# Values spread by transposes, and sums over the features by transposes with row sums on VectorE, in two transformer blocks on one Trainium2 core

## The chip, the cores and the metric

The kernel runs on one core of one Trainium2 chip. The metric is the device time of one execution in microseconds, and less is better. A core has five engines that run their own instruction streams: TensorE (PE in the profile, with its weight loads as PEld), VectorE (DVE), ScalarE (ACT), GpSimd (POOL) and SyncE (SP), which here only starts transfers. TensorE writes only to PSUM, of which this kernel uses eight banks of 128 x 512 fp32.

## The reference

Two blocks run one after the other on x, 512 tokens with 1024 features, in fp32. The first has a forgetting-attention layer and a latent-attention layer, each followed by a squared-ReLU MLP, and a final norm; the second has a mixer with four branches and a gated convolutional feed-forward. What matters for this change are the norms, which all have one shape:

```python
def rms_norm(x, g):
    xf = x.astype(jnp.float32)
    y = xf * lax.rsqrt(jnp.mean(xf * xf, axis=-1, keepdims=True) + EPS)
    return (y * g.astype(jnp.float32)).astype(x.dtype)

def second_block(x, c, ...):
    ...
    h = rms_norm_2(x, tm_pre_g[l]) * (1.0 + sc_t) + sh_t
    y = token_mixer(h, w_in[l], ...)
    x = x + g_t * rms_norm_2(y, tm_post_g[l])
    h = rms_norm_2(x, cm_pre_g[l]) * (1.0 + sc_c) + sh_c
    y = conv_ffn(h, ffn_w_up[l], ffn_dw_w[l], ffn_w_down[l])
    x = x + g_c * rms_norm_2(y, cm_post_g[l])
```

`head_rms_norm`, which the mixer applies to two branches, is the same over groups of 64 features.

## The kernel before

**Layout.** An activation is kept as eight tiles of 128 features x 512 tokens (features on the partitions), and each is split into a high and a low part in fp32r. A product with a weight is three matmuls (`mm3`, lines 215 to 217). The weights come in chunks of 128 x 1024 over SP's queue, are split by ScalarE (L181) and VectorE (L182), and are taken in order by `take`.

**Sums and spreads.** With the features on the partitions, a norm needs a sum over partitions. `token_sum` (L277) has the squares summed over the tiles in one tile `ss` and multiplies each of its 128 x 128 pieces by a tile of ones in plain fp32 (L284): every column of the result holds the sum of 128 tokens, and one column of each piece is read back as 4 values a partition. VectorE scales it (L292), GpSimd takes the power -1/2 (L294). `spread` (L297) brings the 4 values a partition back over all features: a matmul of the broadcast column with the identity (L301), again fp32. `head_rms` (L864, L873) does the sum with a tile that has ones in two 64 x 64 blocks, `head_gain` (L879, L887) the spread for it.

**The mixer.** Its input h is not ready when its first projections start, so these use an earlier h and are corrected by a bias row: `bps`, gathered by L781 in the loop over k, is copied by ScalarE (L804) and turned by four small matmuls (L807). After this come the projections of the short convolution (`sc`), 24 `mm3` matmuls for each of 128 columns, in groups that share the loop over k.

**The start of the second feed-forward.** The tokens are treated in two halves, `HT[0]` and `HT[1]`, with 256-column matmuls in `half_mm`. `half_norms` is a generator: it is advanced by `step(norms)` between two `half_mm`, and does the norm after `w_o` (first `rsqrt_tok`, the residual in L1219 and L1220), the norm before the feed-forward (second `rsqrt_tok`, L1224) and the modulation (`modulate`, L782). `x_tokens` (L1237) turns x to tokens on the partitions by 32 transposes, for the residual at the end.

**Order.** Each engine executes its own instructions in order. The build may place an instruction ahead of others of its engine, so the order of the code is not always that of an engine; where the change speaks of order, rows of it are shown below. PSUM has two pools of four banks, `acc` and `att`; a matmul into a bank waits until the bank's last reader is done.

Of the kernel before, what the change touches and what calls it, by code (L numbers as in the profile page):

```python
# [13 lines left out]
ALU = mybir.AluOpType  # L14
# [5 lines left out]
EPS = 1e-6  # L20
# [66 lines left out]
def _body(ctx, tc, T, n_chunks, rec, dump):  # L87
    nc = tc.nc
    act, dve, pool, pe = nc.scalar, nc.vector, nc.gpsimd, nc.tensor
# [22 lines left out]
    def U(tag="tmp", dt=F32, w=S):  # L112
        if tag in BASE:
            return main.tile([128, w], dt, tag=tag, bufs=BASE[tag], name=tag)
        return phase["pool"].tile([128, w], dt, tag=tag, bufs=phase["tags"][tag], name=tag)
# [4 lines left out]
    def small(w, name="s"):  # L120
        return main.tile([128, w], F32, tag=f"s{w}", bufs=6, name=name)
# [12 lines left out]
    def C(name, w):  # L134
        o = _COFF[name]
        return cst[:, o:o + w]
# [13 lines left out]
    ident = C("ident", 128)  # L150
# [82 lines left out]
    def project(src, cols, X, bank=None):  # L233

        return group(src, [cols], X, bank)[0]

    def group(src, colss, X, bank=None):

        pss = [b() for b in (bank if isinstance(bank, tuple) else (bank or acc,) * len(colss))]
        for k in range(len(X)):  # L240
            for ps, cols in zip(pss, colss):
                wh, wl = take(src, k * 128, cols)
                mm3(ps[0:wh.shape[1]], wh, wl, X[k][0], X[k][1], k == 0, k == len(X) - 1)
        return pss
# [32 lines left out]
    def token_sum(sss):  # L277

        ps = att()
        w = sss[0].shape[1]  # L280
        for s in range(w // 128):
            xs = slice(s * 128, (s + 1) * 128)
            for i, ss in enumerate(sss):
                pe.matmul(ps[:, xs], lhsT=ss[:, xs], rhs=ones, start=i == 0, stop=i == len(sss) - 1)  # L284
        return ps[:, 0:w:128]

    def rsqrt_tok(ss, n, eps=EPS):

        ps = token_sum([ss])
        w = ps.shape[1]  # L290
        t = small(4, "mst")[:, 0:w]
        dve.tensor_scalar(out=t, in0=ps, scalar1=1.0 / n, scalar2=eps, op0=ALU.mult, op1=ALU.add)  # L292
        r = small(4, "rtok")[:, 0:w]
        pool.tensor_tensor(out=r, in0=t, in1=mhalf[:, 0:w], op=ALU.pow)  # L294
        return r

    def spread(rt, tag="tmp"):  # L297

        ps = att()
        for s in range(rt.shape[1]):  # L300
            pe.matmul(ps[:, s * 128:(s + 1) * 128], lhsT=rt[:, s:s + 1].to_broadcast([128, 128]), rhs=ident,  # L301
                      start=True, stop=True)
        if tag is None:
            return ps
        r = U(tag)
        act.activation(out=r, in_=ps, func=AF.Copy)
        return r
# [90 lines left out]
    x, h = [], []  # L398
    for k in range(KT):
        t = U("ctx")  # L400
# [43 lines left out]
    for a in range(2):  # L444
        p0 = 64 - 64 * a
        t = klc[a]
# [167 lines left out]
    ps = acc()  # L614
# [3 lines left out]
    us, ss = mult(pkv, rb2)  # L618
    h = [split_s(x[k], V("norm_mix_g", 8 + k), U2("v" if k < 4 else "h")) for k in range(KT)]
# [20 lines left out]
    us, ss = mult(pq, rb2)  # L640
# [77 lines left out]
    h = []  # L718
# [40 lines left out]
    def ct(name, i):  # L759
        return [(O[name] + 128 * i, 128)]  # L760
# [7 lines left out]
    pss = [acc() for _ in colss]  # L768
# [3 lines left out]
    for k in range(KT):  # L772
# [6 lines left out]
        o = st["slot"] * 128  # L779
# [16 lines left out]
    h = [modulate(k, x[k], rb_h, gG, sh_t, U2("h")) for k in range(KT)]  # L796
    x5d = ctx.enter_context(tc.tile_pool(name="x5d", bufs=1, space=bass.MemoryType.DRAM)).tile([D, S], F32, name="x5d")
    for k in range(KT):
        dve.scalar_tensor_tensor(out=x[k], in0=x[k], scalar=V("final_norm_g", k), in1=rb_f, op0=ALU.mult, op1=ALU.mult)
        nc.scalar.dma_start(out=x5d[k * 128:(k + 1) * 128], in_=x[k])  # L800
        dump(f"x5_{k}", x[k])

    brow = U()
    act.activation(out=brow[0:2], in_=bps[0:2], func=AF.Copy)  # L804
    bps = att()
# [11 lines left out]
    gq, gk = [], []  # L817
    for ps, out, c, b in ((pss[1], gq, 0.125, 10), (pss[2], gk, 1.0, 4), (pss[3], gq, 0.125, 14)):
        t = U("mix")
# [10 lines left out]
    def keep(ps, scale=1.0, tag="tmp"):  # L830
        t = U(tag)
        act.activation(out=t, in_=ps, func=AF.Copy, scale=scale)
        return t
# [30 lines left out]
    def head_rms(hs):  # L864

        t = small(16, "hms")
        for p in range(2):
            ps = att()
            q = U()
            act.activation(out=q, in_=hs[p], func=AF.Square)  # L870
            for s in range(4):
                xs = slice(s * 128, (s + 1) * 128)
                pe.matmul(ps[:, xs], lhsT=q[:, xs], rhs=C("half", 128), start=True, stop=True)  # L873
            dve.tensor_scalar(out=t[:, 8 * p:8 * p + 8], in0=ps[:, 0::64], scalar1=1.0 / 64, scalar2=EPS, op0=ALU.mult, op1=ALU.add)
        r = small(16, "hr")
        pool.tensor_tensor(out=r, in0=t, in1=mhalf, op=ALU.pow)
        return r

    def head_gain(hs, r, gname, gate):  # L879

        out = []
        for p in range(2):
            ps = att()
            re = U()
            dve.tensor_copy(out=re.rearrange("p (a b) -> p a b", a=8), in_=r[:, 8 * p:8 * p + 8].unsqueeze(2).to_broadcast([128, 8, 64]))
            for s in range(4):
                pe.matmul(ps[:, s * 128:(s + 1) * 128], lhsT=re[:, s * 128:(s + 1) * 128], rhs=ident, start=True, stop=True)  # L887
            dve.tensor_tensor(out=hs[p], in0=ps, in1=hs[p], op=ALU.mult)
            dve.scalar_tensor_tensor(out=hs[p], in0=hs[p], scalar=V(gname, p), in1=gate[p], op0=ALU.mult, op1=ALU.mult)
            out.append(split(hs[p], U2("y")))  # L890
        return out
# [8 lines left out]
    for p in range(2):  # L900
        ps = att()
# [6 lines left out]
        scan(gB[p], z, ALU.add)  # L908


    pss = group("w_in_2", [ct("gla_k", 1), ct("sc", 4), ct("sc", 2), ct("sc", 5)], h, (att, att, acc, acc))
    gk.append(keep(pss[0], 1.0, "mix"))
    xv = [keep(pss[1]), keep(pss[3])]
    scu = [ph.tile([128, 2 + S], F32, tag="cv", bufs=2, name=f"scu{p}") for p in range(2)]
    for p in range(2):
        dve.tensor_copy(out=scu[p][:, 0:2], in_=zero[:, 0:2])
    dve.tensor_tensor(out=scu[0][:, 2:], in0=pss[2], in1=xv[0], op=ALU.mult)
    pss = group("w_in_2", [ct("sc", 3), ct("sc", 0), ct("sc", 1)], h)
    dve.tensor_tensor(out=scu[1][:, 2:], in0=pss[0], in1=xv[1], op=ALU.mult)
    yin = {3: []}  # L920
    for p in range(2):
        o = U()
        dve.tensor_scalar(out=o, in0=scu[p][:, 0:S], scalar1=V("sc_dw_w_2", p), scalar2=None, op0=ALU.mult)
        for j in (1, 2):
            dve.scalar_tensor_tensor(out=o, in0=scu[p][:, j:j + S], scalar=V("sc_dw_w_2", 2 * j + p), in1=o, op0=ALU.mult, op1=ALU.add)
        dve.tensor_tensor(out=o, in0=pss[1 + p], in1=o, op=ALU.mult)
        dump(f"sc_{p}", o)
        yin[3].append(split(o, U2("y")))

# [138 lines left out]
    pss = group("w_in_2", [ct("ml_o", 0), ct("ml_o", 1)], h)  # L1068
# [17 lines left out]
    ps = att()  # L1086
# [7 lines left out]
    for p in range(2):  # L1094
        ht = U("misc")
        ps = att()
# [3 lines left out]
        for a in range(2):  # L1100
# [7 lines left out]
                              in1=maskT.unsqueeze(1).to_broadcast([128, 4, 128]), op=ALU.add)  # L1108
            PT = []
            for j in range(4):  # L1110
                n = (4 - j) * 128
# [5 lines left out]
                ps = att()  # L1117
# [7 lines left out]
            ps = att()  # L1125
# [11 lines left out]
    for p in range(2):  # L1137
        o = ph.tile([128, S], F32, tag="cv", bufs=2, name="co")
# [25 lines left out]
    ss = sumsq(co)  # L1164
    gates(1)
    rt = rsqrt_tok(ss, 256)
# [32 lines left out]
    h = [U2("h2") for _ in range(KT)]  # L1199
# [11 lines left out]
    def half_norms(th, ss):  # L1211

        r = rsqrt_tok(ss, D)
        yield
        rb = spread(r, None)
        ss = None
        for k in range(KT):
            y = yt[k][:, th]
            dve.scalar_tensor_tensor(out=y, in0=y, scalar=P_t[:, k:k + 1], in1=rb[:, 0:S // 2], op0=ALU.mult, op1=ALU.mult)  # L1219
            dve.tensor_tensor(out=x[k][:, th], in0=x[k][:, th], in1=y, op=ALU.add)  # L1220
            ss = sq_add(ss, x[k][:, th])
            if k in YA:
                yield
        r = rsqrt_tok(ss, D)  # L1224
        yield
        rb = spread(r, None)
        for k in range(KT):
            modulate(k, x[k][:, th], rb, G_c, sh_c, (h[k][0][:, th], h[k][1][:, th]))
            if k in YB:
                yield  # L1230

    def step(g):
        next(g, None)
# [3 lines left out]
    def x_tokens(s0, s1):  # L1237

        for s in range(s0, s1):
            for g in range(2):  # L1240
                ps = att()
                for k in range(4):
                    pe.transpose(out=ps[:, k * 128:(k + 1) * 128], in_=x[4 * g + k][:, s * 128:(s + 1) * 128], identity=ident)
                xt[g, s] = keep(ps, 1.0, "xt")
# [7 lines left out]
    ss = None  # L1252
# [16 lines left out]
        step(norms)  # L1269
    for _ in norms:  # L1270
        pass
    norms = half_norms(HT[1], ss)


    W, first = [], []
    for i in range(6):
        W.append([take("ffn_w_up_2", k * 128, [((i // 2 + NF2 * (i % 2)) * 128, 128)]) for k in range(KT)])
        first.append(acc() if i < 4 else att())
        half_mm(first[i], W[i], h, HT[0])
        step(norms)  # L1280
        if i == 0:
            step(norms)
    x_tokens(0, 4)
    for _ in norms:
        pass
    for n in range(8):
# [143 lines left out]
```

## Time and profile before

| | before |
|---|---|
| median of 3 runs | 2016.84 us (2015.83 to 2020.51) |
| profiled execution | 2016.43 us |
| its span in the trace | 2014.7 us |
| PE busy | 1982.3 us, 98% |
| DVE busy | 1209.4 us, 60% |
| ACT busy | 878.9 us, 44% |
| mean granted TensorE clock | 0.998 of full |

The span runs from the first to the last instruction in the trace; 1.7 us of the profiled time lie outside it. Busy is the time in which an engine executes an instruction. Matmuls are pipelined, so the distance from one start to the next is what a matmul costs in a stream, and its own duration is longer.

### The profile page before, as it was taken

What the parts mean: (1) busy time and instruction counts of PE and PEld (TensorE: products, weight loads), DVE (VectorE), ACT (ScalarE), POOL (GpSimd) and SP (SyncE); (2) the same over time, 40 slices, a digit from 0 to 9 for tenths busy, and PEclk for the clock granted to TensorE, in tenths of its full rate; (3) what the DMA queues carried; (4) which work ended last, traced back from release to release, by engine and by line L of the source; (5) the groups of instructions that cost most, each with busy time, mean ns of one, the idle gap of its engine ahead of it and who ended that gap; (6) DMA issues with size and microseconds to landing.
All of it is one profiled execution on the core that took longest, in us unless ns stands there. A gap on an engine that the chain in (4) does not pass through costs nothing.

```text
span 2014.7 us, 24990 instructions
## 1 busy us (share of the span) xinstructions
PE 1982.3 (98%) x9726; PEld 1649.3 (82%) x9726; DVE 1209.4 (60%) x1969; ACT 878.9 (44%) x1429; POOL 94.6 (5%) x101
## 2 busy tenths in 40 slices
PE   8999999999999999999999999999999999999998
PEld 6877888888888788888888878788888988888887
DVE  5688665345446985633554577975735576634564
ACT  5688544124334654431333364435523454423341
POOL 0345000000000000000000000000000000000000
PEclk9999999999999999999999999999999999999999
DMA  5221354345233113633543332122222422332331
GB/s 179 76 63 44 114 188 137 97 144 177 95 97 108 53 43 94 220 97 102 174 140 97 97 122 84 64 84 84 74 84 94 147 64 80 97 96 94 100 113 61
DMA packets 61063, 210.32 MB, mean 104 GB/s; under 512 B 6912, under 2 KB 7184, under 8 KB 60944
## 3 DMA queue, kind: packets, MB, share of 16 engines
q1 hardware_dynamic: 56304, 199.99, 31.0%
q10 hardware_dynamic: 4640, 8.73, 1.4%
q8 instruction: 76, 1.25, 0.3%
q14 instruction: 43, 0.35, 0.1%
HBM read 204.50 MB, written 4.19 MB: 104 GB/s over the span
## 4 chain that ended last, share of the span: by engine, by line
PE 88%; DVE 8%; ACT 2%; issue 1%; POOL 0%; DMA 0%; ACTq 0%; DVEq 0%; POOLq 0%; SPq 0%
PE acc L215 23%; PE acc L216 23%; PE acc L217 23%; PE acc L1325 2%; PE acc L1327 2%; PE acc L1326 2%; PE att L215 2%; PE att L216 2%; PE att L217 2%; PE att L373 1%; DVE wl L182 1%; PE acc L257 1%; PE acc L258 1%; PE acc L259 1%; PE att L301 1%
## 5 line engine op out<-in xcount | busy, mean ns | idle before, releaser
L182 DVE TENSOR_TENSOR wl<-wraw,wh 128x1024 fp32r<-128x1024 f32 x312 | 381.7, 1223 | 379.7 <-ACT wh L181 371.1
L181 ACT ACTIVATE wh<-wraw 128x1024 fp32r<-128x1024 f32 x312 | 329.6, 1057 | 616.5 <-PE acc L216 478.6
L215 PE MATMUL acc<-h,wh 128*128 128x512 f32 (+1 forms) x1500 | 577.6, 386 | 1.0 <-DVE vvl L860 1.0
L216 PE MATMUL acc<-h,wh 128*128 128x512 f32 (+1 forms) x1500 | 574.9, 383 | 0.0
L217 PE MATMUL acc<-h,wl 128*128 128x512 f32 (+1 forms) x1500 | 574.7, 383 | 0.0
L215 PEld LDWEIGHTS acc<-h,wh 128*128 128x128 f32 x1500 | 282.1, 188 | 55.6 <-DVE vvl L860 1.2
L217 PEld LDWEIGHTS acc<-h,wl 128*128 128x128 f32 x1500 | 281.9, 188 | 54.7
L216 PEld LDWEIGHTS acc<-h,wh 128*128 128x128 f32 x1500 | 282.1, 188 | 53.2 <-DVE h L230 0.4
L215 PE MATMUL acc<-a,wh 128*128 128x512 f32 x512 | 199.2, 389 | 0.0
L217 PE MATMUL acc<-a,wl 128*128 128x512 f32 x512 | 199.2, 389 | 0.0
L216 PE MATMUL acc<-a,wh 128*128 128x512 f32 x512 | 199.2, 389 | 0.0
L217 PEld LDWEIGHTS acc<-a,wl 128*128 128x128 f32 x512 | 96.1, 188 | 20.0
L215 PEld LDWEIGHTS acc<-a,wh 128*128 128x128 f32 x512 | 96.1, 188 | 20.0
L216 PEld LDWEIGHTS acc<-a,wh 128*128 128x128 f32 x512 | 96.1, 188 | 19.9
L529 DVE CUSTOM_DVE_ANT_0 wada<-wada,ca 128x1024 f32<-128x1024 f32 x48 | 58.8, 1225 | 44.2 <-DMA wada<-in_adaT_dram 42.3
L547 ACT ACTIVATE tmp<-acc 128x512 f32<-128x512 f32 x64 | 37.6, 588 | 99.9 <-PE acc L217 99.4
L561 DVE TENSOR_TENSOR tmp<-acc,rb 128x512 f32<-128x512 f32 x32 | 22.1, 691 | 78.3 <-PE acc L217 78.3
L1292 DVE SCALAR_TENSOR_TENSOR u<-acc,vec,u 128x511 f32<-128x511 f32 x42 | 31.4, 750 | 59.9 <-ACT u L1291 59.9
L294 POOL TENSOR_TENSOR rtok<-mst,mhalf 128x4 f32<-128x4 f32 (+1 forms) x12 | 11.4, 954 | 1113.4 <-DVE mst L292 1113.4
L336 POOL TENSOR_SCALAR P<-P,rs 128x128 f32<-128x128 f32 (+3 forms) x56 | 60.2, 1092 | 30.2 <-DVE rs L356 30.2
L350 ACT ACTIVATE P<-att,mn 128x128 f32<-128x128 f32 (+1 forms) x96 | 50.4, 527 | 23.8 <-DVE mn L347 21.2
L1291 ACT ACTIVATE u<-acc,vec 128x512 f32<-128x512 f32 x42 | 28.7, 683 | 70.3 <-PE acc L217 70.3
(493 smaller groups left out, 3024.1 us busy)
## 6 DMA issues: line engine op xcount, KB each, us to landing
wraw<-in_ws_dram SPq DMA_DIRECT2D x325, 512.0 KB, 3.5
wada<-in_adaT_dram SPq DMA_DIRECT2D x48, 512.0 KB, 3.9
x<-in_xT_dram ACTq DMA_DIRECT2D x8, 256.0 KB, 3.0
x5d<-x ACTq DMA_DIRECT2D x8, 256.0 KB, 2.0
x<-x5d ACTq DMA_DIRECT2D x8, 256.0 KB, 3.6
out_dram<-xt SPq DMA_DIRECT2D x8, 256.0 KB, 2.0
ctx<-in_xT_dram SPq DMA_DIRECT2D x7, 256.0 KB, 5.9
ca<-in_c_dram ACTq DMA_DIRECT2D x2, 512.0 KB, 4.1
```

Of the source, the lines that this page charges most:

```text
L181: act.activation(out=h, in_=w, func=AF.Copy)
L182: dve.tensor_tensor(out=l, in0=w, in1=h.bitcast(F32), op=ALU.subtract)
L215: pe.matmul(ps, lhsT=wh, rhs=xh, start=start, stop=False)
L216: pe.matmul(ps, lhsT=wh, rhs=xl, start=False, stop=False)
L217: pe.matmul(ps, lhsT=wl, rhs=xh, start=False, stop=stop)
L336: pool.tensor_scalar(out=Ps[i], in0=Ps[i], scalar1=rs[:, i:i + 1], scalar2=None, op0=ALU.mult)
L350: act.activation(out=p, in_=ps[:, 0:n], func=AF.Exp, scale=-1.0, bias=mn, accum_out=sume[:, i:i + 1])
L529: dve.tensor_tensor_reduce(out=w, in0=w, in1=ca["t"], scale=1.0, scalar=0.0, op0=ALU.mult, op1=ALU.add, accum_out=mod[:, i:i + 1])
L547: act.activation(out=t, in_=ps, func=AF.Relu)
L1325: pe.matmul(ps, lhsT=a[0][:, xs], rhs=wh, start=k == 0, stop=False)
L1326: pe.matmul(ps, lhsT=a[0][:, xs], rhs=wl, start=False, stop=False)
L1327: pe.matmul(ps, lhsT=a[1][:, xs], rhs=wh, start=False, stop=k == 10)
```

## The change

`token_sum` of one tile becomes `turned_sum`: four transposes bring the tokens to the partitions, and VectorE sums each row of 128. `head_rms` uses the same with 8 sums of 64, and scales both halves at once. `spread` and `head_gain` use transposes in place of products with the identity. `token_sum` of two tiles (16 matmul records before) stays as it is. Besides, one projection of the mixer (`gla_k`, 1) moves ahead of the bias row's matmuls, and the groups of the short convolution are cut differently: before 4 and 3 columns of 128, now 1, 1, 4 and 1. In the second feed-forward `half_norms` has one more `yield`, ahead of its second sum, the steps are spread as (2, 1, 0, 1, 1, 1) over the six `half_mm`, and `x_tokens` is called in two parts, one ahead of the six and one before the fifth step.

```diff
         ps = att()
         w = sss[0].shape[1]
+        if len(sss) == 1:
+            return turned_sum(ps[:, 0:w], sss[0], small(4, "tsum")[:, 0:w // 128])
         for s in range(w // 128):
...
+    def turned_sum(ps, ss, out):
+
+        for s in range(ss.shape[1] // 128):
+            xs = slice(s * 128, (s + 1) * 128)
+            pe.transpose(out=ps[:, xs], in_=ss[:, xs], identity=ident)
+        n = out.shape[1]
+        dve.tensor_reduce(out=out, in_=ps.rearrange("p (n w) -> p n w", n=n), axis=mybir.AxisListType.X, op=ALU.add)
+        return out
...
         for s in range(rt.shape[1]):
-            pe.matmul(ps[:, s * 128:(s + 1) * 128], lhsT=rt[:, s:s + 1].to_broadcast([128, 128]), rhs=ident,
-                      start=True, stop=True)
+            pe.transpose(out=ps[:, s * 128:(s + 1) * 128], in_=rt[:, s:s + 1].to_broadcast([128, 128]), identity=ident)
...
+    gk1 = project("w_in_2", ct("gla_k", 1), h, att)
     brow = U()
     act.activation(out=brow[0:2], in_=bps[0:2], func=AF.Copy)
...
-            for s in range(4):
-                xs = slice(s * 128, (s + 1) * 128)
-                pe.matmul(ps[:, xs], lhsT=q[:, xs], rhs=C("half", 128), start=True, stop=True)
-            dve.tensor_scalar(out=t[:, 8 * p:8 * p + 8], in0=ps[:, 0::64], scalar1=1.0 / 64, scalar2=EPS, op0=ALU.mult, op1=ALU.add)
+            turned_sum(ps, q, t[:, 8 * p:8 * p + 8])
+        dve.tensor_scalar(out=t, in0=t, scalar1=1.0 / 64, scalar2=EPS, op0=ALU.mult, op1=ALU.add)
...
             for s in range(4):
-                pe.matmul(ps[:, s * 128:(s + 1) * 128], lhsT=re[:, s * 128:(s + 1) * 128], rhs=ident, start=True, stop=True)
+                pe.transpose(out=ps[:, s * 128:(s + 1) * 128], in_=re[:, s * 128:(s + 1) * 128], identity=ident)
...
-    pss = group("w_in_2", [ct("gla_k", 1), ct("sc", 4), ct("sc", 2), ct("sc", 5)], h, (att, att, acc, acc))
-    gk.append(keep(pss[0], 1.0, "mix"))
-    xv = [keep(pss[1]), keep(pss[3])]
+    gk.append(keep(gk1, 1.0, "mix"))
+    xv = [keep(project("w_in_2", ct("sc", 4), h, att))]
+    pss = group("w_in_2", [ct("sc", 2), ct("sc", 5), ct("sc", 3), ct("sc", 0)], h)
+    xv.append(keep(pss[1]))
...
-    pss = group("w_in_2", [ct("sc", 3), ct("sc", 0), ct("sc", 1)], h)
...
+    pss = [pss[3], project("w_in_2", ct("sc", 1), h)]
...
             if k in YA:
                 yield
+        yield
         r = rsqrt_tok(ss, D)
...
+    x_tokens(0, 2)
     norms = half_norms(HT[1], ss)
...
         half_mm(first[i], W[i], h, HT[0])
-        step(norms)
-        if i == 0:
+        if i == 4:
+            x_tokens(2, 4)
+        for _ in range((2, 1, 0, 1, 1, 1)[i]):
             step(norms)
-    x_tokens(0, 4)
```

On TensorE, at the bias row of the mixer, the order before: the last two matmuls of `bps` (L781) are followed at once by the bias row's own (L807).

```order
L217 MATMUL acc<-h,wl 128x512
L781 MATMUL att<-wh,shl 2x512
L781 MATMUL att<-wl,shl 2x512
L807 MATMUL att<-cst,tmp 128x2 x4
L215 MATMUL acc<-h,wh 128x512
```

In the change, on the same engine at the same place (L791 and L818 are the lines L781 and L807 of before), the 24 matmuls of `gla_k` stand between them, of which the first three and the last three are shown.

```order
L791 MATMUL att<-wh,shl 2x512
L791 MATMUL att<-wl,shl 2x512
L215 MATMUL att<-h,wh 128x512
L216 MATMUL att<-h,wh 128x512
L217 MATMUL att<-h,wl 128x512
...
L217 MATMUL att<-h,wl 128x512
L818 MATMUL att<-cst,tmp 128x2 x4
L215 MATMUL acc<-h,wh 128x512
```

What moved is the projection: the bias row's matmuls now stand 24 matmuls later.

On TensorE in the second feed-forward, at the second sum of `HT[1]`, before: the sum (L284) is followed at once by the spread (L301), whose input goes through VectorE and GpSimd first. The fourth `half_mm` ends ahead of it and the fifth begins behind it.

```order
L217 MATMUL acc<-h_13019,a 128x256
L284 MATMUL att<-cst,tmp 128x128 x2
L301 MATMUL att<-cst,rtok 128x128 x2
L215 MATMUL att<-h_13005,a 128x256
L216 MATMUL att<-h_13006,a 128x256
```

In the change (L293 is the sum's transpose, L312 the spread's, L1254 the transpose of `x_tokens`), with all but four of the fifth `half_mm`'s 24 matmuls left out:

```order
L217 MATMUL acc<-h_13039,a 128x256
L293 MATMUL att<-cst,tmp 128x128 x2
L215 MATMUL att<-h_13025,a 128x256
L216 MATMUL att<-h_13026,a 128x256
...
L216 MATMUL att<-h_13040,a 128x256
L217 MATMUL att<-h_13039,a 128x256
L1254 MATMUL att<-cst,x 128x128 x16
L312 MATMUL att<-cst,rtok 128x128 x2
L215 MATMUL att<-h_13025,y_13642 128x256
```

Between the sum and its spread there are now 24 matmuls and 16 transposes, where there was nothing. The sum itself still stands behind the fourth `half_mm`. Between the first spread of `HT[1]` and this sum stand 59 matmuls in the change and 51 before; between the second sum of `HT[0]` and its spread 14 in the change and 6 before.

On VectorE, at the first sum of `HT[1]`, the change has the row sum (L295), its scaling (L303), and two of the subtractions that make the low parts of h (L803, L793 before) around the first instruction that waits for the spread (L1229, L1219 before). `h_13037` to `h_13040` are the last two of the eight h of `HT[0]`.

```order
L295 TENSOR_REDUCE tsum<-att 128x2
L802 CAST h_13037<-tmp 128x256
L303 TENSOR_SCALAR mst<-tsum 128x2
L803 TENSOR_TENSOR h_13038<-tmp,h_13037 128x256
L1229 SCALAR_TENSOR_TENSOR xt<-xt,Pg_8870,att 128x256
L803 TENSOR_TENSOR h_13040<-tmp,h_13039 128x256
L1230 TENSOR_TENSOR x<-x,xt 128x256
```

Before, all eight subtractions stood ahead of the scaling there; now two stand behind it, and the last of them behind L1229.

## Rows read from the trace of the kernel before

**Rows 1.** The page: busy time and instructions of each engine.

```profile
PE 1982.3 (98%) x9726; PEld 1649.3 (82%) x9726; DVE 1209.4 (60%) x1969; ACT 878.9 (44%) x1429; POOL 94.6 (5%) x101
```

**Rows 2.** Waits of TensorE: us in total, times, longest.

```profile
PE att L301 <- POOL rtok L294: 2.9, 4, 1.1
...
PE att L807 <- ACT tmp L804: 1.6, 1, 1.6
...
PE acc L215 <- DVE vvl L860: 1.0, 1, 1.0
```

**Rows 3.** By source line: matmuls of sums and spreads, ns min/median/max.

```profile
L284 PE MATMUL att<-cst,tmp x88: 270/275/377, 22.0 to 1649.9; 128*128 128x128 f32 x88
...
L301 PE MATMUL att<-cst,rtok x64: 270/275/578, 24.4 to 1652.1; 128*128 128x128 f32 x64
...
L301 PE MATMUL att<-cst,rt x16: 271/275/348, 272.5 to 808.5; 128*128 128x128 f32 x16
...
L301 PE MATMUL att<-cst,Pg x16: 273/275/276, 1582.9 to 1584.5; 128*128 128x128 f32 x16
...
L301 PE MATMUL att<-cst,rr x8: 270/275/275, 1157.4 to 1158.2; 128*128 128x128 f32 x8
...
L301 PE MATMUL att<-cst,mu x8: 271/275/276, 1497.9 to 1498.7; 128*128 128x128 f32 x8
...
L873 PE MATMUL att<-cst,tmp x32: 270/275/377, 1315.0 to 1477.8; 128*128 128x128 f32 x32
...
L887 PE MATMUL att<-cst,tmp x32: 270/275/276, 1330.9 to 1490.5; 128*128 128x128 f32 x32
```

**Rows 4.** The timeline: a sum and a spread, and what starts behind.

```profile
1149.30 2.05 PE L284 MATMUL att<-cst,tmp 128*128 128x128 f32 x16
1151.11 0.47 PE L781 MATMUL att<-wh,shl 128*2 128x512 f32 x1
...
1157.42 1.05 PE L301 MATMUL att<-cst,rr 128*128 128x128 f32 x8
1158.31 1.06 PE L301 MATMUL att<-cst,rtok 128*128 128x128 f32 x8
```

**Rows 5.** By source line and timeline: the transposes of `x_tokens`.

```profile
L1243 PE MATMUL att<-cst,x x32: 271/273/330, 1659.1 to 1664.3; 128*128 128x128 f32 x32
...
1659.10 1.03 PE L1243 MATMUL att<-cst,x 128*128 128x128 f32 x8
1659.89 0.36 PE L215 MATMUL acc<-h,wh 128*128 128x256 f32 x1
...
1661.23 1.15 PE L1243 MATMUL att<-cst,x 128*128 128x128 f32 x8
1662.14 0.37 PE L215 MATMUL acc<-h,wh 128*128 128x256 f32 x1
```

**Rows 6.** The timeline in the second feed-forward: waits stand in brackets.

```profile
1629.44 0.71 PE L301 MATMUL att<-cst,rtok 128*128 128x128 f32 x4 [0.82 <-POOL rtok L294]
...
1640.60 0.87 DVE L1219 SCALAR_TENSOR_TENSOR xt<-xt,Pg,att 128x256 f32<-128x256 f32 x2 [1.58 <-PE att L301]
...
1646.27 0.28 PE L216 MATMUL acc<-h,a 128*128 128x256 f32 x1
1646.39 0.28 PE L217 MATMUL acc<-h,a 128*128 128x256 f32 x1
1649.49 0.68 PE L284 MATMUL att<-cst,tmp 128*128 128x128 f32 x4 [2.83 <-DVE tmp L268]
...
1651.27 1.23 PE L301 MATMUL att<-cst,rtok 128*128 128x128 f32 x4 [1.10 <-POOL rtok L294]
```

**Rows 7.** Stretches: busy us (instructions) of PE, PEld, DVE, ACT, POOL, granted clock, DMA share, GB/s.

```profile
1651.30:1655.00 3.70, 3.70 (x18) 3.70 (x19) 2.38 (x8) 1.95 (x5) 0.00 (x0) 0.55 0.00 0
...
1659.10:1664.30 5.20, 5.20 (x45) 4.63 (x43) 0.43 (x1) 4.17 (x8) 0.00 (x0) 1.00 0.02 3
```

**Rows 8.** By source line: VectorE reading a whole PSUM bank.

```profile
L561 DVE TENSOR_TENSOR tmp<-acc,rb x32: 683/691/692, 360.7 to 1146.1; 128x512 f32<-128x512 f32 x32
```

More of the change, by code (lines that the diff above doesn't have):

```diff
@@ L916, in _body @@
         dve.tensor_copy(out=scu[p][:, 0:2], in_=zero[:, 0:2])
-    dve.tensor_tensor(out=scu[0][:, 2:], in0=pss[2], in1=xv[0], op=ALU.mult)
-    pss = group("w_in_2", [ct("sc", 3), ct("sc", 0), ct("sc", 1)], h)
-    dve.tensor_tensor(out=scu[1][:, 2:], in0=pss[0], in1=xv[1], op=ALU.mult)
+    for p in range(2):
+        dve.tensor_tensor(out=scu[p][:, 2:], in0=pss[2 * p], in1=xv[p], op=ALU.mult)
+    pss = [pss[3], project("w_in_2", ct("sc", 1), h)]
     yin = {3: []}
@@ L925, in _body @@
             dve.scalar_tensor_tensor(out=o, in0=scu[p][:, j:j + S], scalar=V("sc_dw_w_2", 2 * j + p), in1=o, op0=ALU.mult, op1=ALU.add)
-        dve.tensor_tensor(out=o, in0=pss[1 + p], in1=o, op=ALU.mult)
+        dve.tensor_tensor(out=o, in0=pss[p], in1=o, op=ALU.mult)
         dump(f"sc_{p}", o)
```

## The prediction

> **What bounds the kernel now.** I read the page's busy times first. TensorE is busy for 1982.3 us of a span of 2014.7 and VectorE for 60% of it [rows 1], so TensorE waits for 32.4 us in all, and time is to be had in two ways: fewer or cheaper matmuls, or fewer of those 32 us. Next I read TensorE's waits by the tile waited for. The change touches three of them [rows 2]: spreads wait 2.9 us for `rtok`, the bias row's matmuls 1.6 us for ScalarE's copy, and a matmul of the short convolution 1.0 us for a bank that VectorE still reads. A fourth stands in the timeline of the second feed-forward: the second sum of `HT[1]` starts after 2.83 us without work, and its spread after 1.10 us more [rows 6]. [...]
>
> **What the transposes save.** The trace lists a plain fp32 product twice. A spread of 4 pieces stands there as 8 records, and the rows of the sums and spreads that change have 88 + 64 + 16 + 16 + 8 + 8 + 32 + 32 = 264 records [rows 3], which are 132 matmuls of two passes each. In a stream a pass costs 0.113 us in a sum (16 passes from 1149.30 to 1151.11) and 0.111 in a spread (8 from 1157.42 to 1158.31) [rows 4]. The kernel already has fp32 transposes of 128 x 128, in `x_tokens`: its 32 transposes leave 32 records [rows 5], so one pass each. Eight of them took 0.79 us from the first to what starts behind (1659.10 to 1659.89), and another eight 0.91 (1661.23 to 1662.14), that is 0.099 and 0.114 us each. A transpose therefore costs what one pass of a product costs, and each of the 132 saves the other pass. With 0.110 us, between the two kinds of row, this is 132 x 0.110 = **-14.5 us**, with 0.099 it is -13.1, with 0.114 -15.0.
>
> [...]
>
> **What the row sums add.** VectorE gets 19 of them: 11 of 128 x 512 in `token_sum`, 4 in `head_rms` and 4 of half the width. No row shows this operation. Its cost lies above nothing and I bound it above by VectorE's 0.69 us over a whole bank [rows 8], which reads as many elements from PSUM; that is the value I take, since it is the nearest in shape. 19 x 0.69 is at most 13 us on an engine with 800 us to spare, so it matters only where a sum, its root and its spread follow each other with TensorE waiting. At the start of the mixer and in the other norms of the mixer and the first block's MLPs, the order has matmuls between sum and spread, and the waits list has no entry for their spreads. The exception is the first layer: the four waits for `rtok` are 0.82 and 1.10 in the second feed-forward [rows 6], and 0.98 together elsewhere. The transposes shorten the sum ahead by half of what the row sum adds, so I take **+0.3 us** there, between 0 and 0.7. Were the cover gone at all 15 wide sums, it would be 15 x 0.69 = 10 us.
>
> **The bias row.** Its 1.60 us wait for the copy of `bps` [rows 2] has now 24 matmuls of 512 columns in front, some 5.5 us at twice the 0.12 us of 256 columns. The copy needs 1.6 us, so the wait goes: **-1.6 us**. Behind the bias row stands the rest of the mixer, which starts later by 5.5 us of work that was to be done anyhow; nothing is late that is not late before. The new cut of the short convolution (1, 1, 4, 1 columns) wants four banks of `acc` at once, and its last column alone must find one free. The present wait of this kind is 1.0 [rows 2], so I take **+0.5**, between 0 and 1.0 more.
>
> **The second feed-forward.** The chain in question begins on VectorE with L1219 at 1640.60 and ends with the squares, upon which the sum starts at 1649.49 [rows 6]: 8.9 us, of which 51 matmuls at 0.12 (the last starts at 1646.39) cover 6.1. In the change 59 matmuls, 7.1 us, stand there, 1.0 more, and VectorE has one subtraction of the low parts behind L1219, some 0.3 us more. The wait of 2.83 becomes 2.2. The wait of 1.10 at the spread goes: between the sum and it stand now 24 matmuls (2.9 us) and 16 transposes (1.8), and what the spread needs is a root and a row sum, under 2.5 us. The 0.82 us wait at 1629.44 has 14 matmuls in front in place of 6 (1.0 us) but also a row sum and a queued square (0.9), and stays near 0.7; of the remaining 0.3 nothing changes. From 5.0 us, waiting falls to 3.2: **-1.8 us**. If VectorE's chain grows as much as its cover, this is -1.1, and if the cover suffices, -3.9.
>
> The clock comes on top. The stretch at 0.55 took 3.70 us for what takes 18 x 0.12 = 2.2 at the upper level, so 1.5 us are to be won. What the engine did before was 2.83 us without work, one sum, and 1.10 us without work; behind the 1.60 us wait at the bias row no fall is in the rows. The remaining 2.2 us lie between, so I count about half: **-0.7**, with 0 and -1.5 as ends.
>
> **The sum.** -14.5 - 1.6 - 1.8 - 0.7 + 0.5 + 0.3 = -17.8 us. The profiled execution has 2016.43 us, 2014.7 of it in the span, and the median is 0.4 above it; against the median this gives 2016.84 - 17.8 = **1999.0 us**. With all ends low it is 13.1 + 1.6 - 1.0 - 0.7 + 1.1, or -14.1 (2002.7), with all ends high 15.0 + 1.6 + 3.9 + 1.5, or -22.0 (1994.8).
>
> **Rivals.** *The freed time becomes waiting.* Half of what TensorE saves comes back because VectorE or ScalarE, with longer chains, sets the pace between sum and spread: -7.3 for the passes, -1.6 at the bias row, nothing in the feed-forward, +0.8, so -8.1 and 2008.7. For it speaks that TensorE waits for VectorE in three of the places named; against it that 32 us of waiting in 2015 leave most groups covered, and VectorE is idle 40%.
>
> *The clock falls behind each group of transposes*, and the kernel is slower. The place is the stretch behind each of the some 16 changed norms; the price is that of the one fall in the rows, 3.70 us at 0.55, so 1.7 us lost. All 16 give +27 us, and 2016.8 - 17.8 + 27 = 2026. It decides from 11 falls on, where 1.7 x 11 eats the gain. Against it: 32 transposes among 45 instructions in 5.2 us ran at a granted clock of 1.00 [rows 7], and behind them no slower stretch follows. [...] In rows 7 the transposes stand in groups of eight between matmuls, and the clock holds there; the groups of this change are of 4 to 16, also between matmuls.
>
> *The transposes bring nothing.* If a transpose whose input is a broadcast column, or one of a square, takes two passes like the product, only the small terms remain, -1.6 - 1.8 - 0.7 + 0.8 = -3.3, and 2013.5. The records of `x_tokens` speak against it, which take a full fp32 tile in one pass.
>
> *A transpose takes half a pass.* Then each of the 132 saves another 0.055 us, 7.3 in all, and the sum ends at 1991.7. Nothing in the rows is that short: the quickest eight took 0.099 us each [rows 5]. [...]
>
> **How the numbers follow.** 0.76 for my sum, 0.14 for the freed time as waiting, 0.04 for the clock, 0.04 for transposes that bring nothing, 0.02 for the half pass. 0.2% of this kernel, 4 us, is about what a measurement can tell from no change. The first two cases and the last are faster by more, the third slower, the fourth within it: 0.92, 0.04 and 0.04. The sum's own range is 1994.8 to 2002.7. Since it rests on the pace of other transposes, I widen it to 1993.5 below, and above to 2008.5, up to the middle of the second case.
>
> **What would show it.** Right: sums and spreads (but for the two-tile sum's 16) stand with 132 records in place of 264, at 0.27 us each and about 0.11 apart; TensorE's busy time is 14 to 17 us less; the bias row's matmuls do not wait; the last sum in the feed-forward waits about 2.2 us and its spread not at all; a row sum takes 0.7 us or less. Wrong: TensorE's busy time falls but its idle time grows beyond 32 us, at spreads that wait for `rtok`; the granted clock is under 1.00 behind transposes; or a transpose has two records.

## The result, and the profile after

The changed kernel takes 2003.47 us (median of 6 runs, 2000.83 to 2007.17), the kernel before 2016.34 (6 runs beside them): a ratio of 0.9933, 95% interval 0.992 to 0.9946. Six more runs, with 29 of the kernel before on another occasion, gave 2003.21 and a ratio of 0.9919 (0.99 to 0.9938). It is faster, by 13 to 16 us; 1999.0 was forecast, with a range up to 2008.5. The times of both kernels scatter more than I had allowed for, and most of what follows is about that.

The page of the changed kernel, busy time by engine, first of its first profiled execution (2004.9 us), then of a second one (2000.41 us):

```profile
PE 1974.2 (99%) x9594; PEld 1637.2 (82%) x9594; DVE 1216.8 (61%) x1984; ACT 878.5 (44%) x1429; POOL 97.9 (5%) x101
```

```profile
PE 1968.9 (99%) x9594; PEld 1633.1 (82%) x9594; DVE 1216.7 (61%) x1984; ACT 878.6 (44%) x1429; POOL 97.8 (5%) x101
```

TensorE executes 9726 - 9594 = 132 records fewer than in [rows 1], as forecast. By source line, the sums of one tile and the spreads of `rtok`, which answer to [rows 3]; and the row sums on VectorE, which had no row before:

```profile
L293 PE MATMUL att<-cst,tmp x60: 269/272/328, 21.2 to 1642.1; 128*128 128x128 f32 x60
...
L312 PE MATMUL att<-cst,rtok x32: 270/273/323, 23.9 to 1648.6; 128*128 128x128 f32 x32
...
L295 DVE TENSOR_REDUCE tsum<-att x13: 414/681/693, 21.8 to 1642.4; 128x4 f32<-128x512 f32 x9, 128x2 f32<-128x256 f32 x4
L295 DVE TENSOR_REDUCE hms<-att x4: 678/678/691, 1315.0 to 1473.9; 128x8 f32<-128x512 f32 x4
```

A row sum takes 0.68 us, close to the 0.69 of [rows 8], and there are 17 of them (I had counted 19). TensorE's waits, against [rows 2]:

```profile
PE att L312 <- POOL rtok L305: 2.4, 4, 1.0
...
PE att L293 <- DVE tmp L268: 1.9, 1, 1.9
PE att L312 <- DVE rt L550: 1.5, 2, 0.7
...
PE att L215 <- ACT c L229: 1.4, 1, 1.4
```

The bias row's 1.6 and the 1.0 for the short convolution's bank are gone. Two have grown: the spreads of the squared-ReLU layers wait 1.5 us for `rt`, and the latent attention 1.4 for `c`. The kernel before has for the same two:

```profile
PE att L215 <- ACT c L229: 0.6, 1, 0.6
...
PE att L301 <- DVE rt L540: 0.2, 1, 0.2
```

What I had not expected is the clock. Four stretches of the first trace, in columns as in [rows 7]:

```profile
659.00:664.00 5.00, 4.94 (x15) 3.92 (x16) 3.12 (x6) 1.11 (x3) 0.00 (x0) 0.66 0.05 20
1257.00:1264.00 7.00, 7.00 (x44) 5.29 (x43) 5.54 (x16) 2.38 (x6) 3.13 (x4) 0.52 0.01 4
1301.00:1305.00 4.00, 4.00 (x52) 3.12 (x40) 3.35 (x9) 0.66 (x2) 0.00 (x0) 0.57 0.02 4
1642.50:1647.00 4.50, 4.50 (x28) 4.50 (x27) 0.52 (x2) 0.00 (x0) 0.70 (x1) 0.62 0.00 0
```

In each of them the clock falls to 0.50 of full for 3 to 6 us: behind the latent attention's wait (660 to 663), twice in the mixer's scans (1258 to 1264 and 1302 to 1305), and at the last sum of the second feed-forward (1643 to 1646). In the trace before only the last of these is there (0.50 from 1652 to 1654). At the very end of the program, where TensorE executes nothing, the clock is 0.50 too, from 2010 us on in the trace before and from 2002 on in the first trace after; that is not counted here. The second trace of the changed kernel has a mean clock of 0.999. As an estimate from that, at most one such fall of 3 to 4 us is left in it: (1 - clock) x time is 9.4 us in the first trace, 1.7 of it at the last sum and 0.8 at the end, and 0.999 of 1998.5 us stands for 1 to 3. That makes the second trace the one to hold against [rows 1]: busy time -13.4 us (14.5 forecast), time without work 29.6 in place of 32.4, -2.8 (2.6 forecast), the span 1998.5 in place of 2014.7, -16.2.

### The profile page after: what moved, and what is told of

Same layout as the page of the kernel before. It is cut to its first block, busy times and chain, and to the rows that moved or that the text cites. A ratio compares the mean times of both kernels' runs of the same rounds, so it can differ in the third digit from the quotient of the medians.

```text
span 2003.0 us, 24744 instructions
## 1 busy us (share of the span) xinstructions
PE 1974.2 (99%) x9594; PEld 1637.2 (82%) x9594; DVE 1216.8 (61%) x1984; ACT 878.5 (44%) x1429; POOL 97.9 (5%) x101
## 4 chain that ended last, share of the span: by engine, by line
PE 89%; DVE 6%; ACT 2%; issue 1%; POOL 1%; DMA 0%; DVEq 0%; ACTq 0%; POOLq 0%; SPq 0%
PE acc L215 23%; PE acc L216 23%; PE acc L217 23%; PE acc L1337 2%; PE acc L1339 2%; PE acc L1338 2%; PE att L215 2%; PE att L216 2%; PE att L217 2%; PE att L383 1%; DVE wl L182 1%; PE acc L257 1%; PE acc L258 1%; PE acc L259 1%; PE att L504 0%
## 5 line engine op out<-in xcount | busy, mean ns | idle before, releaser
L539 DVE CUSTOM_DVE_ANT_0 wada<-wada,ca 128x1024 f32<-128x1024 f32 x48 | 58.8, 1224 | 41.1 <-DMA wada<-in_adaT_dram 39.4
L305 POOL TENSOR_TENSOR rtok<-mst,mhalf 128x4 f32<-128x4 f32 (+1 forms) x12 | 14.5, 1205 | 1106.4 <-DVE mst L303 746.3
```

The costliest lines, as they stand in the source:

```text
L539: dve.tensor_tensor_reduce(out=w, in0=w, in1=ca["t"], scale=1.0, scalar=0.0, op0=ALU.mult, op1=ALU.add, accum_out=mod[:, i:i + 1])
```

## The experiments

**How runs are compared.** Each run has a mean granted clock. In 78 runs of the kernel before it went from 0.999 to 0.992, and the time with it, from 2014.91 to 2025.92 us: the 25 runs at 0.998 took 2015.9 on average, the 16 at 0.995 2021.3, the 16 at 0.993 2023.8. A straight line through these runs, against (1 - clock) x span, has a slope of 0.80, which is 1.6 us for 0.001 of clock. "At equal clock" below is the average distance of a kernel's runs from that line, with standard errors of 0.1 to 0.3 us; the mean of the times stands beside it (the mean of the kernel before is 2019.6). Behind the first six runs, the kernels ran on three occasions. The kernel before ran on each of them, with mean clocks of 0.9953 to 0.9962 and within 0.2 us of the line. The row of the sums leaves out one run, of 7264.33 us.

| kernel | runs | mean us | mean clocks | at equal clock |
|---|---|---|---|---|
| changed | 12 | 2003.3 | 0.994 to 0.999 | -15.4 |
| transposes only | 12 | 2014.9 | 0.990 to 0.996 | -9.2 |
| sums only | 11 | 2017.4 | 0.994 to 0.997 | -2.4 |
| spreads only | 12 | 2015.4 | 0.991 to 0.997 | -7.2 |
| order only | 12 | 2013.7 | 0.996 to 0.998 | -4.1 |
| changed, bias row back | 9 | 2010.8 | 0.991 to 0.995 | -11.9 |
| changed, early transposes | 6 | 2001.7 | 0.995 to 0.998 | -17.2 |
| the same with power -1 | 6 | 2000.4 | 0.997 to 0.999 | -16.1 |

**The theories.** Theory 1: a transpose saves a pass, and the clock falls in some runs wherever TensorE is thinly fed, whoever feeds it. Theory 2: the transposes bring the falls (the rival of the prediction). Theory 3: the new order brings them.

**Both kernels again, unchanged.**

> The changed kernel as it is, for a second trace and more runs. Theory 1: 2001 to 2007 us, each run's time set by its mean clock (2.0 us for 0.001), and the falls at other places than the four of the first trace, or another number of them. Theories 2 and 3: the falls at the same four places (behind the latent attention's norm, twice or thrice in the mixer's scans, at the last sum of the second feed-forward) in this trace too.

> The kernel before as it is, for a second trace and for the mean clock of each run. Theory 1: times from 2015.7 to 2020.5 go with mean clocks from 0.998 down to about 0.996, so falls beyond the one of the first trace are there without a single transpose in a sum or spread. Theories 2 and 3: mean clock 0.998 in every run, and the scatter of the times has another cause.

The changed kernel took 1998.66 to 2007.18, and by the mean clock of its trace, 0.999, at least three of the four falls of the first trace were gone; 0.001 of clock goes with 1.6 us and not the 2.0 expected. The kernel before took 2015.54 to 2024.15 with clocks from 0.998 to 0.993, so its own scatter goes with the clock, without a single transpose in a sum or spread. The falls change from run to run of one program, which theory 3 doesn't allow either. The trace of `before_again` is of a run at 0.998, like the first trace of this kernel, so a third execution was traced:

> The kernel before once more, one look, for the places of its falls. Theory 1: where the mean clock is below 0.997, falls stand at places like those of the changed kernel (behind the bias row, in the mixer's scans near 1255 and 1300, at the last sum), though no sum or spread is a transpose; with 0.998 only the one at the last sum.

This run took 2023.46 us, at 0.993. Four stretches of it:

```profile
1178.00:1182.00 4.00, 4.00 (x11) 2.59 (x10) 3.92 (x8) 1.84 (x3) 0.00 (x0) 0.57 0.35 95
1263.50:1271.00 7.50, 7.50 (x45) 5.53 (x45) 7.10 (x17) 3.94 (x8) 3.39 (x4) 0.54 0.21 70
1308.00:1315.00 7.00, 7.00 (x43) 5.29 (x43) 5.69 (x15) 2.19 (x5) 0.00 (x0) 0.51 0.01 2
1656.00:1663.00 7.00, 5.90 (x29) 5.77 (x28) 4.57 (x15) 3.80 (x9) 0.69 (x1) 0.51 0.00 0
```

The first stands behind the bias row, the next two in the scans, the last behind the last sum. These are the changed kernel's places, but for the bias row, where the changed kernel no longer waits, and the latent attention, where it waits longer. That TensorE is thinly fed ahead of a fall, as theory 1 has it, is not shown at the first place in the scans: in the first trace of the changed kernel TensorE is busy for 3.85 of the 4 us from 1253 to 1257, at a clock of 1.00, and in the next two the clock is 0.60 and 0.50.

**Transposes in a row.**

```diff
-                    pe.transpose(out=ps[...], in_=x[4 * g + k][...], identity=ident)
+                    for _ in range(8 if s0 == 0 else 1):
+                        pe.transpose(out=ps[...], in_=x[4 * g + k][...], identity=ident)
```

> The changed kernel with each of the first 16 transposes of x to tokens (those ahead of the second feed-forward's first matmuls) issued eight times into the same place: 128 transposes in a row on TensorE, with nothing between. Theory 1 (a transpose costs one pass of a product, and the clock holds in it): 112 more at 0.110 us, 12.3 us longer than the changed kernel, granted clock 1.00 through the stretch. Theory 2 (transposes do not count as work for the clock): the clock falls to about 0.5 inside or right behind the stretch, and the 128 take 20 us or more. [...]

Two rows of the timeline, and the stretch:

```profile
1621.73 13.37 PE L1255 MATMUL att<-cst,x 128*128 128x128 f32 x121
1634.86 0.36 PE L215 MATMUL acc<-h,wh 128*128 128x256 f32 x1
```

```profile
1621.50:1635.00 13.50, 13.50 (x126) 13.50 (x125) 5.53 (x18) 6.68 (x15) 0.00 (x0) 1.00 0.18 62
```

The first of these rows begins behind the first seven of the 128. The 121 transposes in it took 13.13 us, 0.1085 each, and the granted clock stayed at 1.00 through 13.5 us of little else. Theory 2 falls in this form. The measured price is one of the product's two passes of 0.111 to 0.113 [rows 4], half the price of a product. The run took 2010.48 us; less 112 x 0.1085 it is 1998.3, like the changed kernel at 0.999 (1998.66 and 2000.41).

**Parts of the change, from the kernel before.** Transposes in all sums and spreads and nothing else; then in the sums alone, and in the spreads alone.

```diff
+            return turned_sum(ps[:, 0:w], sss[0], ...)
...
-            pe.matmul(ps[...], lhsT=rt[...].to_broadcast([128, 128]), rhs=ident, start=True, stop=True)
+            pe.transpose(out=ps[...], in_=rt[...].to_broadcast([128, 128]), identity=ident)
```

> The kernel before with transposes and row sums in all sums and spreads, and nothing else of the change. Theory 1 (transposes save a pass each; the clock falls now and then wherever TensorE is thinly fed, whoever feeds it, at 1.7 us a fall): 132 records fewer, about 13 to 15 us faster than before at equal mean clock, and falls at places far from the transposes. Theory 2 (the transposes bring the falls): mean clock about 0.995 in its runs against 0.998 before, only 8 to 10 us faster, falls right behind sums and spreads. Theory 3 (the new order brings the falls): mean clock 0.998 in all runs, 14 us faster.

> The kernel before with transposes and row sums in the sums alone (60 of the 132), spreads as products, order as before. If the row sums are what exposes the chains (row sum 0.68 us, in the chain between sum and spread): waits for the second layers' spreads about 1.3 us longer in all, the bias row's 0.5 longer, the latent attention's 0.8 longer, so 6.6 us saved and some 3 to 4 given back, 3 us net at equal clock. If the shorter cover does it: waits as before, 6 us net.

> The kernel before with transposes in the spreads alone (72 of the 132), sums as products, order as before. If the row sums expose the chains: waits as before, 7.9 us saved, 7 to 8 net at equal clock. If the shorter cover does it: some 2 to 3 us of it turn into waiting. Theory 2 on the clock: mean clocks as low as with all transposes (0.990 to 0.996); theory 1: as before (0.993 to 0.999).

At equal clock the transposes bring -9.2, not the 13 to 15 that theory 1 gave them. The mean clock of 0.993 is as low as theory 2 had it, but the slower stretch that its rows show stands where `before_third` has one, behind the bias row: from 1179.58 to 1182.57 us a matmul of 512 columns starts every 0.43 us, and every 0.23 from 1182.91 on. The 132 records are gone, but waits have come, in this kernel's list:

```profile
PE att L312 <- POOL rtok L305: 4.4, 5, 1.6
PE att L293 <- DVE tmp L268: 3.3, 1, 3.3
PE att L817 <- ACT tmp L814: 2.1, 1, 2.1
```

`rt` and `c` are waited for as in the changed kernel, 1.5 and 1.4 us. Against [rows 2 and 6] the three lines are 1.5 + 0.5 + 0.5 us more, and `rt` and `c` 1.3 + 0.8: 4.6 us. The sums alone give 2.4 of their 6.6, and theirs are the waits for `rt` (1.5) and `rtok` (4.4); the spreads alone give 7.2 of 7.9. So the transposed sums expose the chains of the norms, and the shorter cover costs little there. At the bias row it is the other way round, which I had put to the row sums: its wait is as before with the sums alone, and longer with the spreads alone.

```profile
PE att L818 <- ACT tmp L815: 1.6, 1, 1.6
```

```profile
PE att L806 <- ACT tmp L803: 2.1, 1, 2.1
```

Both kernels with transposed spreads in the old order ran at lower clocks (means of 0.993 and 0.994 against 0.996), and here I had expected, by theory 1, no difference. A row of transposes as such is out as a cause: the burst held 1.00. That the bias row's wait of 2.1 in place of 1.6 us gives more falls fits the means of all these kernels: 0.996 and 0.997 where it does not wait (changed, order only), 0.996 where it waits 1.6 us (before, sums only), 0.993 and 0.994 at 2.1. The next but one experiment bears on it.

**The order alone.** The changed kernel with products in all sums and spreads.

> The changed kernel with plain products in all sums and spreads again, so that only the order differs from before (bias row, cut of the short convolution, second feed-forward). Theory 1: 3 to 4 us faster than before at equal mean clock, the mean clock scattered from 0.994 to 0.998 from run to run. Theory 2 (transposes bring the falls): mean clock 0.998 in all runs, 4 us faster. Theory 3 (the order brings the falls): mean clock about 0.995, no faster than before or slower by up to 3 us.

-4.1 at equal clock, 3 to 4 expected; the clocks lie in a narrower band, 0.996 to 0.998, so theory 3 falls here too, and theory 2's 0.998 in every run does not come either. Transposes and order add up to -13.3, and together they make -15.4: the order is worth 6.2 behind the transposes and 4.1 without, because it covers waits that the transposes lengthen. The lists of waits bear this out: at the last sum, the bias row, `rtok` and the short convolution's bank the order takes away 0.9 + 1.6 + 0.6 + 1.0 = 4.1 us without the transposes, and 1.4 + 2.1 + 2.0 + 1.0 = 6.5 behind them.

**The bias row.** The projection that was moved ahead goes back.

```diff
-    gk1 = project("w_in_2", ct("gla_k", 1), h, att)
     brow = U()
...
+    gk1 = project("w_in_2", ct("gla_k", 1), h, att)
     gk.append(keep(gk1, 1.0, "mix"))
```

> The changed kernel with the projection of gla_k behind the bias row's matmuls again; transposes, cut of the short convolution and second feed-forward as changed. Theory 1 (what TensorE waits for sets both the time and where the clock can fall): the bias row waits about 2.1 us again, 1.6 to 2.1 us longer at equal mean clock, and in part of the runs falls right behind that wait, so that the mean clock is lower than the changed kernel's and the mean time 3 to 6 us longer. Rival (the wait costs its length alone): 1.6 to 2.1 us longer, clocks as in the changed kernel.

The mean is 7.5 us longer, 3.5 at equal clock, both more than expected, and no run of nine is above 0.995, where the changed kernel's twelve, from two other occasions, have 0.994 to 0.999. The timeline at the bias row and the stretch around it, here, and then both in the changed kernel:

```profile
1172.57 1.05 PE L817 MATMUL att<-cst,tmp 2*128 2x2 f32 x8 [2.05 <-ACT tmp L814]
1174.37 0.80 PE L215 MATMUL acc<-h,wh 128*128 128x512 f32 x1 [0.75 <-ACT wh L181]
```

```profile
1174.00:1185.00 11.00, 10.63 (x21) 6.24 (x22) 4.49 (x9) 8.13 (x14) 0.00 (x0) 0.53 0.26 95
```

```profile
1177.69 1.05 PE L818 MATMUL att<-cst,tmp 2*128 2x2 f32 x8
```

```profile
1174.00:1185.00 11.00, 11.00 (x47) 7.83 (x46) 7.43 (x13) 6.49 (x10) 0.00 (x0) 1.00 0.57 184
```

The wait is 2.05, a second one of 0.75 for split weights follows, which I had not expected, and the mean clock over the 11 us is 0.53: 21 instructions where the changed kernel executes 47. Moving this one projection is nearly half of the change's gain in the mean, 7.5 of 16.3 us. Whether the lower clock is due to the length of the first wait or to the two together is not shown.

**A version that fills the last wait.** The 16 transposes of `x_tokens(2, 4)` stand ahead of the last sum.

```diff
-        if i == 4:
+        if i == 3:
             x_tokens(2, 4)
```

> The changed kernel with the second part of the transposes of x to tokens ahead of the second feed-forward's last sum in place of behind it, so that they stand where TensorE waits 1.9 us. The wait falls to 0.3 us or less, no fall of the clock behind it: 1.6 us from the wait, and 1.7 us where the fall was, 2 to 3.5 us faster than the changed kernel in its mean. If the spread behind is uncovered by it (24 matmuls, 2.9 us, stand between): up to 1 us back. If x is not ready in time, no change.

The timeline, first of the changed kernel from the second sum's spread of `HT[0]` on, then of this one at the last sum:

```profile
1622.02 0.43 PE L312 MATMUL att<-cst,rtok 128*128 128x128 f32 x2 [0.68 <-POOL rtok L305]
...
1632.48 0.43 PE L312 MATMUL att<-cst,rtok 128*128 128x128 f32 x2 [0.51 <-POOL rtok L305]
...
1641.98 0.41 PE L293 MATMUL att<-cst,tmp 128*128 128x128 f32 x2 [1.90 <-DVE tmp L268]
...
1648.47 0.40 PE L312 MATMUL att<-cst,rtok 128*128 128x128 f32 x2
```

```profile
1640.49 1.91 PE L1254 MATMUL att<-cst,x 128*128 128x128 f32 x16
...
1642.54 0.44 PE L293 MATMUL att<-cst,tmp 128*128 128x128 f32 x2
...
1645.73 0.38 PE L312 MATMUL att<-cst,rtok 128*128 128x128 f32 x2
```

The wait is gone, the spread does not wait, and no slower stretch stands there: the 23 matmuls from 1642.98 on start every 0.12 us, where in the first trace of the changed kernel they start every 0.21 from 1642.96 to 1646.16. The mean is 1.6 us below the changed kernel's, 1.8 at equal clock: the 1.6 expected for the wait came, and the 1.7 for the fall did not, since the mean clock of the six runs, 0.9962, is that of the changed kernel's twelve. Its ratio to the kernel before, 0.9906 (0.9887 to 0.9925), overlaps with the changed kernel's.

**The same with a shorter chain** in the two squared-ReLU layers.

```diff
-        rt = rsqrt_tok(sumsq(x), D)
-        rt2 = small(4, "rt2")
-        dve.tensor_tensor(out=rt2, in0=rt, in1=rt, op=ALU.mult)
-        r2 = spread(rt2, tag="rb")
+        r2 = spread(rsqrt_tok(sumsq(x), D, power=mone), tag="rb")
```

> The kernel with the early transposes of x, and in the two squared-ReLU layers GpSimd takes the power -1 in place of -1/2, so that VectorE's squaring between it and the spread goes (one small instruction and its queue). If the spreads' two waits of 0.72 us are the chain's end through VectorE: they fall to about 0.3 each, 0.8 to 1 us faster than the kernel with the early transposes at equal clock, about 2001 in the mean. If TensorE is held up there by something else: no change.

This missed. The build placed the spread earlier, 8 matmuls behind the sum in place of 13, so TensorE waits longer for the shorter chain, 1.64 us in place of 0.72:

```profile
270.21 1.88 POOL L307 TENSOR_TENSOR rtok<-mst,mone 128x4 f32<-128x4 f32 x1 [66.96 <-DVE mst L305]
272.15 0.65 PE L314 MATMUL att<-cst,rtok 128*128 128x128 f32 x4 [1.64 <-POOL rtok L307]
```

At equal clock it is 1.1 us behind the version before it. Its mean of 2000.4 is the lowest of all, because none of its six runs was under 0.997; six runs don't tell whether that is the kernel or chance.

## Why the prediction came out as it did

*The passes.* Right: 132 records fewer, 0.1085 us a transpose, and 13.4 us of busy time in the two traces at 0.998 and 0.999, between the ends of 13.1 and 15.0. The sign "14 to 17 us less" busy time was not met, neither by these 13.4 nor by the 8.1 of the first trace.

*The row sums.* Priced rightly (0.68 us) and placed wrongly. The step that failed is "the waits list has no entry for their spreads", from which +0.3 us followed. The list has one, 0.2 us for `rt`; the first layer's spread gave the +0.3 (0.7 to 1.0), but `rt` added 1.3 and `c` 0.8. A list without a wait says nothing of how much cover is left. VectorE's rows at the latent attention show what the 0.68 leaves out:

```profile
648.78 0.68 DVE L295 TENSOR_REDUCE tsum<-att 128x4 f32<-128x512 f32 x1
649.38 1.21 DVE L182 TENSOR_TENSOR wl<-wraw,wh 128x1024 fp32r<-128x1024 f32 x1
650.51 1.32 DVE L223 TENSOR_TENSOR v<-acc,v 128x512 fp32r<-128x512 f32 x2
651.75 0.16 DVE L303 TENSOR_SCALAR mst<-tsum 128x4 f32<-128x4 f32 x1
```

Where one instruction of VectorE stood between sum and root, there are now two, and 2.3 us of other work is queued between them. At the squared-ReLU layers the price of the row sum is not the whole of it either. There GpSimd's power, the next step of the chain, takes 1.89 and 1.85 us in place of 1.05 (rows at the end), and the spread behind it waits 0.72 and 0.73. As an estimate from these rows, the matmuls in between would have covered a power of the old length.

```profile
272.48 0.65 PE L312 MATMUL att<-cst,rt 128*128 128x128 f32 x4 [0.72 <-DVE rt L550]
```

*The bias row.* The wait went, as said. Against the kernel before, that is the 1.6 of the forecast. Behind transposes it is worth 3.5 at equal clock, of which the rows show the 2.05 that the wait would have been, and 0.75 for the weights behind it. The step "behind the 1.60 us wait at the bias row no fall is in the rows" was true of that execution and not of the program: the third trace of before has the fall, 0.57 from 1178 to 1182. The cut of the short convolution, taken at +0.5, took its wait of 1.0 away.

*The second feed-forward.* Right in place and size: the last sum's wait went from 2.83 to 1.90 (2.2 forecast), its spread's 1.10 to nothing, the 0.82 to 0.68 (0.7 forecast), and the remaining 0.3 is now 0.51. That is 3.1 us of waiting, and 3.2 were forecast.

*The waiting in all.* It fell by 2.8 us with 2.6 forecast, and that this is so close is luck: `rt` and `c` took 2.1 us more than the sum had for them, the short convolution 1.5 less than it had, and the transposes of P in the attention, which it does not have, wait for ScalarE 0.8 us less (1.8 before, 1.0 after).

*The clock.* This is the term that missed. I counted falls as a fixed property of a wait, one before and half a one after. (The stretch at 0.55 behind this term is the first of [rows 7], and the upper level is a clock of 1.00, as in the second; the 0.12 us is the step from one 256-column matmul to the next in [rows 6], 1646.27 to 1646.39, where it is 1.00.) They come and go from run to run, at some five places. The first trace after happens to have three more such stretches than the trace before, which is why its busy time is only 8.1 us less; on the whole the two kernels ran at about the same clock (0.9963 and 0.9958 on average). The medians of the first six runs fell by 12.9 us, 4.9 less than the forecast 17.8. At equal clock 1.7 of that are missing. The rest is mostly clock: by the line, the six runs of before, at 2016.34, stand for some 0.998, and the changed kernel's had 0.996, which is about 3 us, where -0.7 was forecast.

*The rivals.* The freed time as waiting is the one that had the most in it: with the order of before, 5 of 14.5 us come back, most of it as waits. In the changed order TensorE waits less than before. The slower clock behind transposes did not happen: 1.00 through the 13.5 us of the burst and the 5 behind it. At equal clock the change gives 15.4 us, where the sum without its clock term had 17.1. The measured 2003.47 lies above the sum's own upper end, 2002.7, and inside the range only because that was widened to 2008.5 for the freed time as waiting, which is not what came.

Open is why a longer wait at the bias row should make the clock fall more often, and why the runs of one program differ.

## What to carry to other kernels

Cheaper matmuls around a dependent chain shorten their own cover, and a step added to the chain on another engine needs more of it; here the second cost more. So price the cover that is left at each place, in us, not the wait that is listed, and count every instruction that the chain has in another engine's queue, since the build puts other work between two of them. A wait on TensorE cost its length here, and behind the one at the bias row the clock was lower besides (0.53 over 11 us). So a short projection moved into it can be worth several times the wait, as at the bias row (7.5 us in the mean for 2.05 and 0.75), or just its length, as at the last sum (1.6 for 1.9). With times that scatter by 10 us, look at the mean clock of each run before reading a difference of medians.

## What the runs showed that was not expected

The kernel before alone spans 2014.91 to 2025.92 us with mean clocks from 0.999 to 0.992. GpSimd's power over 128 x 4 took 1.05 us at the first squared-ReLU layer before:

```profile
270.96 1.05 POOL L294 TENSOR_TENSOR rtok<-mst,mhalf 128x4 f32<-128x4 f32 x1 [66.25 <-DVE mst L292]
```

After, it took 1.89, where the new order of VectorE's queue has put it beside the reduction L539 (270.11 to 271.33):

```profile
270.11 1.22 DVE L539 CUSTOM_DVE_ANT_0 wada<-wada,ca 128x1024 f32<-128x1024 f32 x1
...
270.35 1.89 POOL L305 TENSOR_TENSOR rtok<-mst,mhalf 128x4 f32<-128x4 f32 x1 [67.00 <-DVE mst L303]
```

At the second such layer it took 1.85 beside the same instruction, where the kernel before has 1.05 with that reduction done. Over the twelve powers of a trace, the mean is 1.21 to 1.25 us in six traces with transposed sums, and 0.94 to 1.03 in the five with products in the sums. That the one slows the other was not tested by itself.
